# Moving the right-hand SBUF pools of a hybrid encoder layer by 160 bytes

## The chip, the cores and the metric

The kernel runs on one core of a Trainium2 chip. The metric is the device time of one execution in microseconds (us). The time before is 2487.82 us, the median of three runs (2487.3 to 2491.13 us).

## What is computed

One encoder layer on x of 1024 tokens and 1024 channels, all in float32. An RMSNorm is followed by one wide projection (10,016 columns of `w_in`, 1024 rows); its columns feed three branches, each a scan in both directions: a state-space branch (SSD), an RWKV-7 branch and an HGRN2 branch. Each branch is projected to 1024 channels, the three are merged with sigmoid gates, and an output projection and a residual addition follow. Then come RMSNorm, a SwiGLU feed-forward part with 2816 inner channels, another residual addition and a last RMSNorm.

```python
p = rmsnorm(x, norm1_w) @ w_in
z, xbc, dt_raw, p_rwkv, p_hgrn, p_gate = split(p)
mixed = g0 * (ssd(...) @ w_branch_ssm) + g1 * (rwkv7(...) @ w_branch_rwkv) + g2 * (hgrn2(...) @ w_branch_hgrn)
x = x + mixed @ w_out
h_gate, h_up = split(rmsnorm(x, norm2_w) @ ffn_w_in)
x = x + (silu(h_gate) * h_up) @ ffn_w_down
out = rmsnorm(x, final_norm_w)
```

## The kernel before

**A product in three matmuls.** Every large float32 product is made of three fp32r matmuls. Each operand is split into a high part (a cast on ACT) and a low part (the difference, on DVE or POOL), and high times high, high times low and low times high are added up in PSUM. `mm3` (L226 to L232), `Jobs.steps` (L329 to L331) and `rows_mm` (L1572 to L1578) issue them. In `matmul(ps, a, b)` the first operand is loaded into TensorE as weights, 128 columns, and the second streams through it, 512 columns. In the profile, a matmul `out<-in,in` names the streaming operand first.

**Stages.** Until about 1500 us the scans run, with the first projections filling TensorE between them (`Jobs`, which the FILL table portions out; its matmuls are L329 to L331). Then:
- merges (`merges`, L1461 on): branch projections, L230 to L232, whose results are gated and added
- output projection (`out_proj`), 384 matmuls, L1576 to L1578, each row group followed by a sum on DVE and a square on ACT; from its second half transposes for the next stage are mixed in (L1601)
- up stage (`Ffn.up`): for each of 22 column blocks f, seven block products (Strassen-Winograd) in the order 1, 2, 6, 7, 5, 4, 3, each of 12 matmuls (L1576 to L1578). The weight blocks are split just ahead of their use (L1740 on ACT, L1741 on DVE), the sums of products go through DVE
- down stage (`Ffn.down`): seven products over six groups of inner channels, 924 matmuls on the same lines. DVE splits the weight blocks and the activation blocks (L1793) and adds each product into an accumulator (L1915); the last group also makes the final norm.

A planner, which simulates the program while it is built, sets the order of the instructions on each engine; a wait is added wherever an instruction touches a buffer that another has to finish with first, also where two pools use the same bytes one after the other.

**Where the operands lie.** SBUF is given out by pools, each with one row of bytes per partition. Pools grow from the left end, or from the right end with `side="right"`. The right end is byte 229,344, which is 224 modulo 256. The pools that hold matmul operands, with their first byte and this modulo 256:

| pool | side | first byte | modulo 256 | holds |
|---|---|---|---|---|
| wpool | left | 20032 | 64 | weights of the projections (wh, wl), raw weights |
| gtp | left | 48704 | 64 | gb blocks of the up stage, raw tiles |
| ring0, ring1 | left | 65088, 97856 | 64 | operands of merges and output projection (oh, ol) |
| ffl | left | 79424 | 64 | xb of products 6, 7, 4 |
| dn | left | 79424 | 64 | ab blocks, accumulators |
| stpool | right | 223552 | 64 | on128 and other masks, staging tiles |
| xpool | right | 158016 | 64 | the normed input x, split |
| r32 | right | 196576 | 224 | rb blocks, gates, two operands of the merges (or) |
| mpool0, mpool1 | right | 163808, 131040 | 224 | mx; then xb of products 1, 2, 5, 3 |

All tiles in these pools that matmuls read have sizes that are multiples of 2048 bytes, and a block inside them starts at a multiple of 512 bytes, so an operand keeps its pool's offset modulo 256. stpool and xpool are closed at the end of the first projections; r32 and the mpools are opened at their place. on128 is a byte mask of 1025 columns, for which 1056 bytes are set aside; all of stpool takes 5792 bytes.

So, before, the weights and the streaming operand meet like this (offset of streaming operand, offset of weights): first projections 64, 64; merges 64, 64, but 224, 64 for `or`; output projection 64, 224; up stage, from the second f on, 224, 64 for products 1 and 2, 64, 224 for products 6, 7 and 4, and 224, 224 for products 5 and 3; down stage 224, 64.

Of the kernel before, what the change touches and what calls it, by code (L numbers as in the profile page):

```python
# [9 lines left out]
F32 = mybir.dt.float32  # L10
F32R = mybir.dt.float32r
U8 = mybir.dt.uint8
# [6 lines left out]
P = 128  # L19
L = 1024  # L20
# [32 lines left out]
def setup_consts(g, tp):  # L53
    nc, A = g.nc, g.A
    cp = g.cpool
    ident = cp.tile([P, P], F32, tag="ident", name="ident")
    nc.gpsimd.memset(ident, 1.0)
    nc.gpsimd.affine_select(out=ident, in_=ident, pattern=[[1, P]], compare_op=ALU.is_equal,
                            fill=0.0, base=0, channel_multiplier=-1)
    g.ident = ident  # L60

    def tri(name, op, base, cm, step, scale=1.0):
        t = cp.tile([P, P], F32, tag=name, name=name)
        nc.gpsimd.memset(t, scale)
        nc.gpsimd.affine_select(out=t, in_=t, pattern=[[step, P]], compare_op=op, fill=0.0,
                                base=base, channel_multiplier=cm)
        return t

    g.tri = tri
    g.tri_le = tri("tri_le", ALU.is_ge, 0, -1, 1)  # L70
    g.tri_ge = tri("tri_ge", ALU.is_ge, 0, 1, -1)


    bd = tp.tile([P, P], F32, tag="bd", name="bd")
    nc.gpsimd.memset(bd, 0.0)
    nc.gpsimd.memset(bd[0:64, 0:64], 1.0)
    nc.gpsimd.memset(bd[64:128, 64:128], 1.0)
    ones = tp.tile([P, P], F32, tag="ones", name="ones")
    nc.gpsimd.memset(ones, 1.0)
    g.bd, g.ones = (cp.tile([P, P], F32R, tag=n, name=n) for n in ("bd", "ones"))  # L80
    nc.gpsimd.tensor_scalar(g.bd, bd, 1.0, None, MUL)
    nc.gpsimd.tensor_scalar(g.ones, ones, 1.0, None, MUL)

    col = cp.tile([P, 8], F32, tag="col", name="col")
    for i, v in enumerate((1.0, NORM_EPS, 1e-12, LN_EPS)):
        nc.gpsimd.memset(col[:, i:i + 1], v)
    g.c_one, g.c_eps, g.c_12, g.c_ln = (col[:, i:i + 1] for i in range(4))

    g.vec = {}


def vector_rows(g, pool, tag, groups, queue):

    out = []
    for gi, grp in enumerate(groups):
        rows = pool.tile([P, P], F32, tag=f"rows{tag}{gi}", name=f"rows{tag}{gi}")
        o = 0
        for name, src, k in grp:
            queue.dma_start(rows[o:o + k, :], src)
            o += k  # L100
        out.append((f"{tag}{gi}", rows, grp))
    return out


def vector_cols(g, loaded):

    nc = g.nc
    for tag, rows, grp in loaded:
        n = sum(e[2] for e in grp)
        ps = g.mmps.tile([P, 512], F32, tag="mm", name="vps")  # L110
        nc.tensor.transpose(ps[:, :n], rows[:n, :], g.ident[:n, :n])
        cols = g.cpool.tile([P, n], F32, tag=f"vcols{tag}", name=f"vcols{tag}")
        nc.vector.tensor_copy(cols, ps[:, :n])
        o = 0
        for name, src, k in grp:
            g.vec[name] = cols[:, o:o + k]
            o += k
# [74 lines left out]
def rms_rows(g, xt, junk, xn, st):  # L192

    nc = g.nc
    nc.scalar.activation(junk, xt, AF.Square, accum_out=st[:, 0:1])
    nc.scalar.activation(st[:, 1:2], st[:, 0:1], AF.Sqrt, bias=g.c_eps, scale=1.0 / D)
    nc.vector.reciprocal(st[:, 0:1], st[:, 1:2])
    nc.vector.tensor_scalar(xn, xt, st[:, 0:1], None, MUL)


def transpose_split(g, x, half, xs, wcols, new, psum=None):

    nc = g.nc
    for k in range(KT):
        ps = (psum or g.mmps).tile([P, 512], F32, tag="mm", name="tps")
        for j in range(4):
            nc.tensor.transpose(ps[:, j * P:(j + 1) * P], xs[j][:, k * P:(k + 1) * P], g.ident)
        hi, lo = new(half, k)
        nc.scalar.activation(hi, ps, AF.Identity, scale=wcols[:, k:k + 1])
        nc.vector.scalar_tensor_tensor(lo, ps, wcols[:, k:k + 1], f32(hi), MUL, SUB)  # L210
        x.add(half, hi, lo)
# [172 lines left out]
def rwkv(g):  # L384
# [38 lines left out]
    with tc.manual_schedule(engines={ACT}):  # L423
        J.first(0)
    derived_vectors(g)
    level_masks(g)

    keep = ExitStack()
# [534 lines left out]
def level_masks(g):  # L963
    nc = g.nc

    on = g.on128 = g.stpool.tile([P, L + 1], U8, tag="on128", name="on128")
    nc.gpsimd.memset(on, 1)
    nc.gpsimd.memset(on[:, 0:L].rearrange("p (c t) -> p c t", t=P)[:, :, 0:1], 0)
    nc.gpsimd.memset(on[:, L:L + 1], 0)


    t2 = g.stpool.tile([P, 3, 64], F32, tag="st", name="blk", bufs=2)
    blk, blk2 = t2[:, 0], t2[:, 1]
    msk = g.msk = g.stpool.tile([P, 6, 64], U8, tag="msk", name="msk")
    g.id64 = g.stpool.tile([P, 64], F32, tag="id64", name="id64")
    for b in range(2):
        nc.gpsimd.tensor_scalar(g.id64[b * 64:b * 64 + 64], g.ident[b * 64:b * 64 + 64, b * 64:b * 64 + 64],
                                1.0, None, MUL)


    def blocks(t, n):
        nc.gpsimd.memset(t, 1.0)
        for b in range(2):
            if n < 64:
                v = t[b * 64:b * 64 + 64].rearrange("p (a b) -> p a b", b=n)

                nc.gpsimd.affine_select(out=v, in_=v, pattern=[[-n, 64 // n], [0, n]], compare_op=ALU.is_ge,
                                        fill=0.0, base=0, channel_multiplier=1)
                nc.gpsimd.affine_select(out=v, in_=v, pattern=[[n, 64 // n], [0, n]], compare_op=ALU.is_ge,
                                        fill=0.0, base=n - 1, channel_multiplier=-1)  # L990
    blocks(blk, 64)
    for i, h in enumerate(LEV[1:]):
        blocks(blk2, h)
        nc.vector.tensor_sub(msk[:, i], blk, blk2)
        nc.vector.tensor_copy(blk, blk2)
# [971 lines left out]
def start(es, tc, A):  # L1967
    g = Ctx()
    g.tc, g.nc, g.A = tc, tc.nc, A
    nc = tc.nc  # L1970
    g.wraw_bufs = 2
    g.lo_eng = nc.gpsimd
    g.wq = nc.scalar
    g.cpool = es.enter_context(tc.tile_pool(name="const", bufs=1))
    g.dram = es.enter_context(tc.tile_pool(name="scr", bufs=1, space=DRAM))
    g.mmes = es.enter_context(ExitStack())
    g.mmps = g.mmes.enter_context(tc.tile_pool(name="mmps", bufs=3, space=PSUM))
    g.wpool = es.enter_context(tc.tile_pool(name="wpool", bufs=2))
    g.xes = es.enter_context(ExitStack())
    g.stpool = g.xes.enter_context(tc.tile_pool(name="stpool", bufs=1, side="right"))  # L1980
    g.xpool = g.xes.enter_context(tc.tile_pool(name="xpool", bufs=1, side="right"))
    x = g.x = Split()

    def new(half, k):
        return [g.xpool.tile([P, 512], F32R, tag=f"x{half}{k}{i}", name="x1") for i in "hl"]

    g.n1 = ExitStack()
    tp = g.n1.enter_context(tc.tile_pool(name="n1", bufs=1))
    nc.scalar.preload_act_table_set("sqrt_and_others")
    xs = [tp.tile([P, D], F32, tag="xt", name="xt", bufs=NT) for _ in range(NT)]  # L1990

    def load(half):
        for t in range(half * 4, half * 4 + 4):
            nc.sync.dma_start(xs[t], A["x"][0, t * P:(t + 1) * P, :])

    def rows(half):
        for t in range(half * 4, half * 4 + 4):
            junk = tp.tile([P, D], F32, tag="junk", name="junk", bufs=2)
            st = tp.tile([P, 2], F32, tag="st", name="st", bufs=4)
            rms_rows(g, xs[t], junk, xs[t], st)  # L2000

    def trans(half):
        with tc.tile_pool(name="n1ps", bufs=4, space=PSUM) as pp:
            transpose_split(g, x, half, xs[half * 4:half * 4 + 4], g.vec["norm1_w"], new, pp)

    g.x_load, g.x_rows, g.x_trans = load, rows, trans
    load(0)
    setup_consts(g, tp)
    n1w = vector_rows(g, tp, "n", [[("norm1_w", A["norm1_w"].rearrange("o (k p) -> (o k) p", p=P), 8)]], nc.scalar)
    vector_cols(g, n1w)  # L2010
    g.n1pool = tp
    return g


@with_exitstack
def layer_kernel(ctx, tc, A, out):
    g = start(ctx, tc, A)
    J = g.J = Jobs(g)

# [101 lines left out]
```

## Time and profile before

| | |
|---|---|
| median of three runs | 2487.82 us |
| the profiled execution | 2489.66 us |
| its span, first to last instruction | 2487.9 us |
| PE busy | 2332.5 us, 94% of the span |
| DVE busy | 1635.9 us, 66% |
| ACT busy | 988.9 us, 40% |
| POOL busy | 1068.9 us, 43% |
| granted TensorE clock, mean | 0.964 of full speed |

PE is TensorE's matmul part and PEld its weight loads, which run beside it; DVE is VectorE, ACT ScalarE, POOL GpSimd. Matmuls are pipelined, and a matmul's end is modelled: its "duration" overlaps the next matmul's, so the rate is read from the starts, or from the number of weight loads in a stretch that is full. The granted clock has two levels, 1.0 (2.4 GHz) and 0.5 (1.2 GHz).

### The profile page before, as it was taken

What the parts mean: (1) busy time and instruction counts of PE and PEld (TensorE: products, weight loads), DVE (VectorE), ACT (ScalarE), POOL (GpSimd) and SP (SyncE); (2) the same over time, 40 slices, a digit from 0 to 9 for tenths busy, and PEclk for the clock granted to TensorE, in tenths of its full rate; (3) what the DMA queues carried; (4) which work ended last, traced back from release to release, by engine and by line L of the source; (5) the groups of instructions that cost most, each with busy time, mean ns of one, the idle gap of its engine ahead of it and who ended that gap; (6) DMA issues with size and microseconds to landing.
All of it is one profiled execution on the core that took longest, in us unless ns stands there. A gap on an engine that the chain in (4) does not pass through costs nothing.

```text
span 2487.9 us, 37793 instructions
## 1 busy us (share of the span) xinstructions
PE 2332.5 (94%) x14785; PEld 1870.3 (75%) x14785; DVE 1635.9 (66%) x2130; ACT 988.9 (40%) x1460; POOL 1068.9 (43%) x862
## 2 busy tenths in 40 slices
PE   8998999999989889999899899999899999999995
PEld 6776788888867677778568667788688888877764
DVE  5688862456566866846666776553774454469999
ACT  6544532222464653436135235332433333344333
POOL 4433422344044533420751761421454444447885
PEclk9998999899999999999899999999999999999998
DMA  5455685655342232225645647531132222253321
GB/s 149 126 145 131 164 209 139 189 164 149 118 138 91 77 109 77 68 88 172 140 125 172 142 128 250 189 115 72 60 102 81 80 84 78 85 172 109 102 67 68
DMA packets 381215, 306.27 MB, mean 123 GB/s; under 512 B 111273, under 2 KB 323149, under 8 KB 381037
## 3 DMA queue, kind: packets, MB, share of 16 engines
q1 hardware_dynamic: 260909, 225.71, 30.6%
q10 hardware_dynamic: 119936, 77.61, 10.7%
q8 instruction: 117, 1.92, 0.3%
q0 software_dynamic: 192, 0.52, 0.1%
q14 instruction: 61, 0.50, 0.1%
HBM read 209.68 MB, written 94.11 MB: 122 GB/s over the span
## 4 chain that ended last, share of the span: by engine, by line
PE 59%; DVE 23%; POOL 5%; issue 5%; DMA 4%; ACT 3%; SPq 0%; ACTq 0%; DVEq 0%; POOLq 0%
PE mm L329 6%; PE mm L330 6%; PE mm L331 6%; PE ps L1577 6%; PE ps L1576 6%; PE ps L1578 6%; DVE acc L1915 3%; DVE ab L1793 2%; PE Gps L802 2%; PE mm L232 2%; PE mm L230 2%; PE mm L231 2%; DMA E<-cumd 2%; POOL E L1357 2%; DVE rb L1793 2%
## 5 line engine op out<-in xcount | busy, mean ns | idle before, releaser
L329 PE MATMUL mm<-x,wh 128*128 128x512 f32 (+1 forms) x1232 | 500.0, 406 | 0.5 <-ACT wh L220 0.5
L330 PE MATMUL mm<-x,wh 128*128 128x512 f32 (+1 forms) x1232 | 497.2, 404 | 0.0
L331 PE MATMUL mm<-x,wl 128*128 128x512 f32 (+1 forms) x1232 | 495.0, 402 | 0.8 <-DVE wl L222 0.7
L329 PEld LDWEIGHTS mm<-x,wh 128*128 128x128 f32 (+1 forms) x1232 | 234.5, 190 | 62.2 <-issue 10.6
L331 PEld LDWEIGHTS mm<-x,wl 128*128 128x128 f32 (+1 forms) x1232 | 234.7, 190 | 57.2 <-issue 6.0
L330 PEld LDWEIGHTS mm<-x,wh 128*128 128x128 f32 (+1 forms) x1232 | 234.8, 191 | 55.9 <-issue 6.8
L1577 PE MATMUL ps<-xb,rb 128*128 128x512 f32 x432 | 171.1, 396 | 0.0
L1576 PE MATMUL ps<-xb,rb 128*128 128x512 f32 x432 | 170.1, 394 | 0.0
L1578 PE MATMUL ps<-xb,rb 128*128 128x512 f32 x432 | 169.9, 393 | 0.0
L220 ACT CAST wh<-wr 128x1024 fp32r<-128x1024 f32 (+2 forms) x103 | 100.3, 974 | 125.1 <-PE mm L330 102.4
L222 POOL TENSOR_TENSOR wl<-wr,wh 128x1024 fp32r<-128x1024 f32 x30 | 78.2, 2606 | 149.2 <-ACT wh L220 140.0
L1576 PE MATMUL ps<-rb,ab 128*128 128x512 f32 x308 | 127.4, 414 | 14.3 <-DVE acc L1915 13.5
L222 DVE TENSOR_TENSOR wl<-wr,wh 128x1024 fp32r<-128x1024 f32 (+2 forms) x73 | 98.1, 1343 | 64.6 <-ACT wh L220 64.5
L1577 PE MATMUL ps<-rb,ab 128*128 128x512 f32 x308 | 125.3, 407 | 2.3 <-POOL rb L1793 2.3
L1578 PE MATMUL ps<-rb,ab 128*128 128x512 f32 x308 | 124.1, 405 | 1.5 <-DVE ab L1793 1.5
L1740 ACT CAST rb<-fs 128x512 fp32r<-128x512 f32 x85 | 52.5, 621 | 172.1 <-PE ps L1578 119.7
L271 ACT COPY st<-mm 128x512 f32<-128x512 f32 x130 | 75.5, 581 | 95.1 <-PE mm L331 76.0
L805 DVE TENSOR_TENSOR Gc<-Gps,mk 128x256 f32<-128x256 f32 x64 | 27.0, 423 | 112.4 <-PE Gps L802 58.6
L1576 PEld LDWEIGHTS ps<-xb,rb 128*128 128x128 f32 x432 | 81.2, 188 | 19.9
L1578 PEld LDWEIGHTS ps<-xb,rb 128*128 128x128 f32 x432 | 81.2, 188 | 19.0
L1577 PEld LDWEIGHTS ps<-xb,rb 128*128 128x128 f32 x432 | 81.1, 188 | 18.9
L1357 POOL TENSOR_TENSOR E<-E,cums 128x1024 f32<-128x1024 f32 x32 | 68.3, 2146 | 60.3 <-DMA E<-cumd 54.5
(503 smaller groups left out, 5584.8 us busy)
## 6 DMA issues: line engine op xcount, KB each, us to landing
wr<-in_w_in_dram ACTq DMA_DIRECT2D x74, 512.0 KB
fr<-in_ffn_w_in_dram SPq DMA_DIRECT2D x44, 512.0 KB
E<-cumd SPq DMA_DIRECT2D x32, 512.0 KB
pg<-st ACTq DMA_DIRECT2D x48, 256.0 KB
gt<-pg SPq DMA_DIRECT2D x24, 512.0 KB
ad<-a SPq DMA_DIRECT2D x22, 512.0 KB
dr<-in_ffn_w_down_dram SPq DMA_DIRECT2D x22, 512.0 KB
ar<-ad SPq DMA_DIRECT2D x22, 512.0 KB
```

What stands on the lines that cost most here:

```text
L220: nc.scalar.copy(hi[:, :kt, :n], raw[:, :kt, :n])
L222: g.lo_eng.tensor_sub(lo[:, :kt, :n], raw[:, :kt, :n], f32(hi[:, :kt, :n]))
L271: g.nc.scalar.copy(st[:n], ps)
L329: g.nc.tensor.matmul(ps[:n], w[0][:, k, :n], xh, start=(k == 0), stop=False)
L330: g.nc.tensor.matmul(ps[:n], w[0][:, k, :n], xl, start=False, stop=False)
L331: g.nc.tensor.matmul(ps[:n], w[1][:, k, :n], xh, start=False, stop=(k == KT - 1))
L1357: nc.gpsimd.tensor_tensor(e, e, cs.unsqueeze(2).broadcast_to([P, 8, P]), SUB)
L1576: nc.tensor.matmul(ps, ah, bh, start=(i == 0), stop=False)
L1577: nc.tensor.matmul(ps, ah, bl, start=False, stop=False)
L1578: nc.tensor.matmul(ps, al, bh, start=False, stop=(i == n - 1))
L1793: eng.tensor_sub(blk[:, 1], s, f32(blk[:, 0]))
L1915: nc.vector.tensor_add(m[j], m[j], ps)
```

## The change

Two edits. A pool of 160 bytes is opened at the right end ahead of all other right-hand pools, and it stays open; one column of it is set to zero by a POOL memset. The mask tile on128 is allocated with 1408 columns instead of 1025, and the first 1025 are used as before.

```diff
@@ def level_masks(g):
-    on = g.on128 = g.stpool.tile([P, L + 1], U8, tag="on128", name="on128")
+    on = g.on128 = g.stpool.tile([P, L + 384], U8, tag="on128", name="on128")[:, 0:L + 1]
     nc.gpsimd.memset(on, 1)
@@ def start(es, tc, A):
     g.wpool = es.enter_context(tc.tile_pool(name="wpool", bufs=2))
+
+    rp = es.enter_context(tc.tile_pool(name="rightpad", bufs=1, side="right"))
+    nc.gpsimd.memset(rp.tile([P, 40], F32, tag="pad", name="pad")[:, 0:1], 0.0)
     g.xes = es.enter_context(ExitStack())
     g.stpool = g.xes.enter_context(tc.tile_pool(name="stpool", bufs=1, side="right"))
     g.xpool = g.xes.enter_context(tc.tile_pool(name="xpool", bufs=1, side="right"))
```

## Rows read from the trace of the kernel before

**Rows 1.** The page: span, busy time of the engines, granted clock in 40 slices.

```profile
span 2487.9 us, 37793 instructions
...
PE 2332.5 (94%) x14785; PEld 1870.3 (75%) x14785; DVE 1635.9 (66%) x2130; ACT 988.9 (40%) x1460; POOL 1068.9 (43%) x862
...
PEclk9998999899999999999899999999999999999998
```

**Rows 2.** Busy time by stretch (start:end, length, busy us and count, clock, DMA).

```profile
66.52:106.05 39.53, 39.53 (x175) 32.67 (x174) 24.17 (x17) 20.78 (x27) 17.95 (x15) 1.00 0.24 64
...
1501.37:1532.91 31.54, 31.54 (x140) 26.09 (x139) 17.41 (x24) 14.19 (x17) 0.00 (x0) 1.00 0.78 277
1570.22:1675.60 105.38, 105.38 (x460) 86.13 (x459) 50.81 (x54) 36.27 (x44) 31.06 (x23) 1.00 0.42 134
1675.69:1736.82 61.13, 61.13 (x263) 49.13 (x262) 20.55 (x33) 12.65 (x30) 7.84 (x5) 1.00 0.24 89
...
1774.48:1804.99 30.51, 23.97 (x93) 17.05 (x92) 30.23 (x36) 16.41 (x29) 19.38 (x12) 0.83 0.18 52
1804.99:2215.52 410.53, 410.53 (x1764) 331.37 (x1763) 214.19 (x303) 128.50 (x212) 183.71 (x130) 1.00 0.28 90
...
2255.00:2415.00 160.00, 151.18 (x608) 116.02 (x607) 159.88 (x189) 57.34 (x103) 133.75 (x86) 0.97 0.30 96
```

The five busy times are those of PE, PEld, DVE, ACT and POOL in this order.

**Rows 3.** The chain that ended last, by line: up stage, then output projection.

```profile
by line: PE ps L1577 33.5%; PE ps L1576 33.3%; PE ps L1578 33.2%
...
by line: PE mm L1576 30.7%; PE mm L1577 30.4%; PE mm L1578 30.0%; PE tps L1601 3.5%; PE ps L1578 1.9%; PE ps L1577 1.8%; PE ps L1576 1.8%
```

**Rows 4.** The same chain in the down stage, 2215 us to the end.

```profile
by line: DVE acc L1915 23.8%; DVE ab L1793 22.8%; DVE rb L1793 14.2%; issue 8.5%; DVE acc L1949 5.4%; POOL dt L1802 4.4%; POOL as L1837 3.2%; POOL acc L1919 3.1%; DVE acc L1954 2.1%; DVE as L1837 2.1%; DMA ar<-ad 1.8%; POOL rb L1793 1.7%; A
```

**Rows 5.** PE in order of time in the up stage: start, length, instruction.

```profile
1886.05 0.40 PE L1576 MATMUL ps<-xb,gb 128*128 128x512 f32 x1
...
1888.85 0.40 PE L1576 MATMUL ps<-xb,rb 128*128 128x512 f32 x1
...
1900.04 0.40 PE L1576 MATMUL ps<-xb,rb 128*128 128x512 f32 x1
...
1901.89 0.39 PE L1578 MATMUL ps<-xb,rb 128*128 128x512 f32 x1
...
1902.80 0.39 PE L1576 MATMUL ps<-xb,gb 128*128 128x512 f32 x1
```

**Rows 6.** PE's groups in the down stage: busy, mean ns, idle before them and releaser.

```profile
L1576 PE MATMUL ps<-rb,ab 128*128 128x512 f32 x308 | 127.4, 414 | 14.3 <-DVE acc L1915 13.5
L1577 PE MATMUL ps<-rb,ab 128*128 128x512 f32 x308 | 125.3, 407 | 2.3 <-POOL rb L1793 2.3
L1578 PE MATMUL ps<-rb,ab 128*128 128x512 f32 x308 | 124.1, 405 | 1.5 <-DVE ab L1793 1.5
```

**Rows 7.** DVE's splits of the up stage by tile: duration min/median/max, first and last start.

```profile
L1741 DVE TENSOR_TENSOR gb<-fr,gb x43: 679/694/1783, 1789.4 to 2163.5; 128x512 fp32r<-128x512 f32 x43
...
L1741 DVE TENSOR_TENSOR rb<-fr,rb x23: 679/693/1783, 1675.9 to 2186.0; 128x512 fp32r<-128x512 f32 x23
```

**Rows 8.** POOL's first instructions in order of time, and the chain's first pieces.

```profile
3.41 0.11 POOL L403 MEMSET pt<- 128x1 f32 x1
3.44 0.11 POOL L404 MEMSET pt<- 128x1 f32 x1
...
2.68 7.73 DMA wr<-in_w_in_dram
...
13.46 1.11 PE tps L207 x4
```

**Rows 9.** PE in order of time in the down stage, around one hole.

```profile
2265.41 0.50 PE L1576 MATMUL ps<-rb,ab 128*128 128x512 f32 x1 [2.54 <-DVE acc L1915]
...
2266.55 0.63 PE L1577 MATMUL ps<-rb,ab 128*128 128x512 f32 x1
...
2269.53 0.50 PE L1578 MATMUL ps<-rb,ab 128*128 128x512 f32 x1
```

## The prediction

> **What bounds the kernel now.** I read the page first: one core, span 2487.9 us in an execution of 2489.66 us, against a median of 2487.82 us of three runs; PE is busy for 94% of the span, and its granted clock is at the full level in nearly every slice [rows 1]. So the kernel is a matmul stream, and the question is where this stream stands still and how fast it goes where it doesn't. The second view, busy time by stretch, answers both [rows 2]. In the up stage of the feed-forward part PE is busy for 410.53 of 410.53 us at full clock, and DVE has half its time free (214.19 us); the chain through that stretch is PE alone, 100% [rows 3]. The two stretches of the merges and the output projection that end at 1736.82 us are full too, and the projection's chain is PE for nine tenths. In the down stage it is the other way round: DVE is busy for 159.88 of 160.00 us and PE has holes; its chain names DVE's accumulations and splits first [rows 2, 4].
>
> Now the rate. All matmuls named here have the same form (128x128 weights, 128x512 columns, fp32r), one weight load each, so the number of weight loads in a stretch counts them. At full clock and without a hole, a matmul takes, from rows 2:
> - first projections, xpool against wpool: 39.53 us / 174 = 227.2 ns
> - merges, ring against wpool: 31.54 / 139 = 226.9 ns
> - output projection, ring against mpool: 61.13 / 262 = 233.3 ns
> - up stage: 410.53 / 1763 = 232.9 ns.
>
> The mean durations of groups (405 to 414 ns [rows 6]) hide this, because pipelined matmuls overlap; only the spacing of the starts tells. Beside it I put the memory map: left-hand pools and xpool start at byte 64 modulo 256, r32 and the two mpools at 224. The fast stretches pair 64 with 64, the slow ones 64 with 224. The up stage holds both kinds in one place: products 1, 2, 6, 7 and 4 pair the two offsets, products 5 and 3 pair 224 with 224. Product 2 of one f goes from 1886.05 to 1888.85 us, 12 matmuls, 233 ns each. Product 3 starts at 1900.04 and the next product at 1902.80: its first eight take 1.85 us (231 ns), its last four 0.91 us (227.5 ns) [rows 5]. So a shared offset gives 227 ns at 224 as well as at 64, and the delay of a mixed pair reaches some matmuls into the next product. I take it that the moving operand of one matmul and the weight load of the next read SBUF at the same time and disturb each other by their relative place.
>
> **The change, part by part.** *Pad.* 160 bytes at the right end put r32 and both mpools 160 bytes lower: 196576, 163808 and 131040 become 196416, 163648 and 130880, all 64 modulo 256. *Wider mask tile.* on128 grows from 1056 to 1408 bytes as allocated, so stpool from 5792 to 6144; with the pad, xpool moves by 512 bytes and stays at 64. The first projections keep their 227 ns, and all pairs above then share 64.
>
> *Up stage:* 1763 x (232.9 - 227.0) = 10.3 us. All of it is on the path, since PE is 100% of the chain; what is late next, DVE, has 196 us in hand.
> *Output projection:* 262 x (233.3 - 227.0) = 1.65 us to 1736.82 us; the remaining 122 of its 384 matmuls lie among transposes in the next stretch, at the same saving 0.8 us. PE holds that chain too.
> *Merges:* 96 matmuls stream two tiles that lie in r32; their stretch gives 105.38 / 459 = 229.6 ns, so 459 x 2.6 = 1.2 us.
> *Stretch from 1774.48 to 1804.99 us:* DVE 30.23 of 30.51 us; a faster matmul gives nothing. Taken at 0.
> *Down stage:* its 924 matmuls pair 224 with 64 and would give 924 x 6.5 = 6.0 us if PE set the pace. It does not: DVE does nearly no waiting, and PE waits 18.1 us for others [rows 2, 6]. A faster matmul makes PE wait longer for DVE's accumulation, which is late next. Between 0 and 6.0 us I take 0.3 us, near the lower end, because the DVE row is full.
> DVE's splits and additions there start when the last up products give their buffers back, so what is saved before 2215 us is not lost at that border.
>
> *Added memset* of one column on POOL: such a memset takes 0.11 us, starts 0.03 us before the next, and stands before the identity that the first transposes need; they start at 13.46 us, behind a weight load from HBM of 7.73 us [rows 8]. Cost nothing; without that cover 0.1 us at most. The mask's memsets still write 1025 bytes. *Buffers at new places:* an r32 tile spanned parts of three xpool tiles and now spans two exactly, so its first load can only wait for fewer readers; bound 0 to 1 us of gain, taken at 0. *DVE, ACT and POOL* on the moved tiles: the split into gb (64) and into rb (224) has a median of 694 and 693 ns [rows 7]; I take 0.
>
> Sum: 10.3 + 1.65 + 0.8 + 1.2 + 0.3 = 14.2 us. From the profiled execution, 2489.66 us, this gives 2475.4; it lies 1.84 us above the median, so from the median 2473.6 us.
>
> One rule speaks against all this. The rows show 233 and 227 ns for one form at one clock. The Trainium skill, "TensorE: Matmul & The Clock Gate", section "Step-by-step: what each phase is for", says that TensorE reads the moving operand and the next weights through two independent ports, so that loading weights takes nothing from the running matmul. By it no address could matter and the sum would be 0. The trace does not agree, 227 against 233 ns.
>
> **Rivals.**
> - *The gain is only partial.* If products in the up stage with one offset stay at the 230 ns that product 3 averages (2.76 us / 12), the up stage gives 1763 x 2.9 = 5.1 us and the rest about half, 1.9 us: 2480.8 us. For: the products at 224 never had a whole 227 ns average. Against: their last four do, and whole stretches at 64.
> - *Nothing changes.* The spacing comes with the stage, not the offset (say, the traffic of the other engines beside it), and the two reads of TensorE do not meet: 2487.8 us. For: the trace shows no address. Against: both rates inside one product sequence of the up stage. This is the outcome that the Trainium skill's page "TensorE: Matmul & The Clock Gate" stands for.
> - *The down stage gains as well*, since DVE is released earlier by each PSUM bank: the other 5.7 us too, 2467.9 us. Against: the full DVE row.
> - *Slower: the clock in the down stage.* With matmuls 6.5 ns shorter, PE's holes grow. After a hole of 2.54 us, ended by DVE at 2265.41, the clock falls, and from 2266.55 to 2269.53 us seven matmuls stand 427 ns apart instead of 234: 1.4 us [rows 9]. The mean clock there is 0.97 now. To end 5 us slower the kernel would need (14.2 + 5) / 1.4, some 14 more such falls; at 17 it would be at 2497 us. Each hole grows by 0.08 us only (12 matmuls), so I hold it for unlikely.
> - The instruction order may also come out differently, as a planner sets it and one POOL instruction is new; the trace can't price this. I let it widen the range.
>
> **How the numbers follow.** Within 0.2% means within 5.0 us, about what a measurement of this kernel can tell from no change. Forecast 0.62, partial 0.15, down stage too 0.07: faster 0.84. No change 0.11. Slower, by the clock or another order, 0.05. The range goes from 2466, just beyond the case with the down stage, to 2483, below which the partial case lies; it leaves out the case of no change and the slower one.
>
> **What would show it.** Right: the up stage at 227 ns, about 400 us for 1763 matmuls; the output projection at 227; the first projections unchanged at 227; the down stage as long as now (272 us from the last up product to the end) with more PE idle behind DVE's accumulation. Wrong: the up stage at 230 or above (partial), any stretch of xpool against wpool off 227 ns, or a down stage longer by microseconds with a lower clock. If the up stage is 400 us and the time still doesn't fall by 12 us, the down stage or a new order took it back.

## The result and the profile after

The changed kernel takes 2472.72 us (median of six runs, 2469.6 to 2476.17), against 2487.69 us before, measured beside it: 15.0 us less, a ratio of 0.9938 with a 95% interval of 0.9925 to 0.9951. The forecast was 2473.6 us.

The profiled execution took 2473.65 us. The page's head, against [rows 1]:

```profile
span 2471.9 us, 37794 instructions
...
PE 2309.0 (93%) x14785; PEld 1865.5 (75%) x14785; DVE 1633.4 (66%) x2130; ACT 989.0 (40%) x1460; POOL 1070.9 (43%) x863
```

One instruction more, the memset; PE is busy for 23.5 us less and its weight loads for 4.8 us less, the other engines within 2.5 us of before. Busy time by stretch comes next, the stretches of [rows 2] at their new times; the columns are PE, PEld, DVE, ACT and POOL, then granted clock and DMA.

```profile
67.90:107.43 39.53, 39.53 (x175) 32.66 (x174) 24.18 (x17) 20.78 (x27) 17.96 (x15) 1.00 0.23 64
1499.53:1531.10 31.57, 31.57 (x140) 26.10 (x139) 17.40 (x24) 14.11 (x17) 0.00 (x0) 1.00 0.78 273
1568.13:1672.52 104.39, 104.39 (x460) 86.40 (x459) 49.48 (x54) 36.27 (x44) 32.27 (x23) 1.00 0.44 137
1672.52:1731.92 59.40, 59.40 (x263) 49.13 (x262) 18.92 (x33) 12.75 (x30) 9.97 (x5) 1.00 0.25 92
1768.93:1799.45 30.52, 24.56 (x93) 17.86 (x92) 30.23 (x36) 16.43 (x30) 19.51 (x13) 0.78 0.18 52
1799.45:2199.06 399.61, 399.61 (x1764) 331.00 (x1763) 215.31 (x303) 128.55 (x212) 183.36 (x129) 1.00 0.29 93
2199.06:2471.94 272.88, 225.38 (x926) 174.74 (x924) 265.58 (x324) 106.34 (x208) 206.28 (x132) 0.94 0.29 99
```

Read each row as length over weight loads. The first projections take 39.53 us for 174 matmuls, to the hundredth what they took before, 227.2 ns. The output projection now needs 59.40 / 262 = 226.7 ns instead of 233.3, the up stage 399.61 / 1763 = 226.7 ns instead of 232.9. PE fills these stretches as before; it is full at a higher rate, and the chain through the up stage is still PE alone:

```profile
by line: PE ps L1576 33.4%; PE ps L1578 33.3%; PE ps L1577 33.3%
```

The last row, the down stage to the end, is within half a microsecond of what it was: 272.88 us, against 272.42 us before, whose row is

```profile
2215.52:2487.94 272.42, 230.76 (x926) 177.01 (x924) 265.16 (x323) 106.23 (x208) 206.77 (x132) 0.93 0.30 99
```

In order of time, the products of the up stage no longer show an uneven spacing. These are the starts around the border of two products:

```profile
1880.60 0.39 PE L1577 MATMUL ps<-xb,gb 128*128 128x512 f32 x1
1880.83 0.39 PE L1578 MATMUL ps<-xb,gb 128*128 128x512 f32 x1
1881.06 0.39 PE L1576 MATMUL ps<-xb,rb 128*128 128x512 f32 x1
1881.28 0.39 PE L1577 MATMUL ps<-xb,rb 128*128 128x512 f32 x1
1881.51 0.39 PE L1578 MATMUL ps<-xb,rb 128*128 128x512 f32 x1
```

Four steps take 0.91 us, across a change from gtp's weights to r32's, where only the last matmuls of a product in [rows 5] were that quick.

Where did the down stage's share go? PE's groups there, which answer to [rows 6]:

```profile
L1576 PE MATMUL ps<-rb,ab 128*128 128x512 f32 x308 | 125.8, 408 | 20.1 <-DVE acc L1915 19.1
L1577 PE MATMUL ps<-rb,ab 128*128 128x512 f32 x308 | 122.4, 397 | 2.4 <-POOL rb L1793 2.4
L1578 PE MATMUL ps<-rb,ab 128*128 128x512 f32 x308 | 121.5, 397 | 1.5 <-DVE ab L1793 1.5
```

The idle time ahead of L1576 rose from 14.3 to 20.1 us, and what ends it is DVE's accumulation, 19.1 us instead of 13.5. PE's busy time in the stage fell from 230.76 to 225.38 us, by 5.4 us, and over the three groups PE waits 24.0 us instead of 18.1, 5.9 us longer: the gain turned into a wait.

Between the profiled executions the books are: scans and first projections 2.1 us shorter (1483.66 to 1481.52 us at the first merge), merges 191.57 to 190.55 (1.0 us), output projection from the end of the merges to 1774.48 us before and 1768.94 us after, 99.26 to 96.86 us (2.4 us), the stretch behind it unchanged, up stage 10.9 us, down stage 0.5 us longer; in sum 16.0 us. The first 2.1 us are not counted for the change: no operand pair there has a new distance, and over the six kernels of this study whose xpool lies at wpool's offset the first merge starts anywhere from 1474.2 to 1483.7 us in the profiles. That leaves 13.9 us for the change, and the interval of the ratio, some 12 to 19 us, holds both them and the 15.0 us of the medians. Of these, the 1.0 us of the merges is the least certain: over the eight kernels of this study that hold the layer, the merges as a whole take 189.8 to 191.6 us in no order of the change; only their full stretch tells, 105.4 to 105.5 us in the three kernels that stream `or` from 224 and 104.0 to 104.6 us in the four in which `or` shares its weights' offset. The planner's order hardly moved: PE's 14785 matmuls come in the same order in both traces, by the names of their tiles, and so do DVE's instructions; on ACT two instructions changed places with a neighbour.

### The profile page after: what moved, and what is told of

Its sections match the earlier page's. It is cut to its first block, busy times and chain, and to the rows that moved or that the text cites. A ratio compares the mean times of both kernels' runs of the same rounds, so it can differ in the third digit from the quotient of the medians.

```text
span 2471.9 us, 37794 instructions
## 1 busy us (share of the span) xinstructions
PE 2309.0 (93%) x14785; PEld 1865.5 (75%) x14785; DVE 1633.4 (66%) x2130; ACT 989.0 (40%) x1460; POOL 1070.9 (43%) x863
## 4 chain that ended last, share of the span: by engine, by line
PE 60%; DVE 23%; POOL 5%; issue 5%; DMA 4%; ACT 3%; ACTq 0%; SPq 0%; DVEq 0%; POOLq 0%
PE mm L329 6%; PE mm L330 6%; PE mm L331 6%; PE ps L1576 6%; PE ps L1577 6%; PE ps L1578 6%; DVE acc L1915 3%; DVE ab L1793 2%; PE Gps L802 2%; PE mm L232 2%; PE mm L230 2%; PE mm L231 2%; DMA E<-cumd 2%; POOL E L1357 2%; DVE rb L1793 1%
## 5 line engine op out<-in xcount | busy, mean ns | idle before, releaser
L329 PEld LDWEIGHTS mm<-x,wh 128*128 128x128 f32 (+1 forms) x1232 | 234.1, 190 | 61.7 <-issue 10.6
L1578 PE MATMUL ps<-xb,rb 128*128 128x512 f32 x432 | 168.1, 389 | 0.0
L1576 PE MATMUL ps<-xb,rb 128*128 128x512 f32 x432 | 168.0, 389 | 0.0
L1577 PE MATMUL ps<-xb,rb 128*128 128x512 f32 x432 | 168.0, 389 | 0.0
L1576 PE MATMUL ps<-rb,ab 128*128 128x512 f32 x308 | 125.8, 408 | 20.1 <-DVE acc L1915 19.1
L1577 PE MATMUL ps<-rb,ab 128*128 128x512 f32 x308 | 122.4, 397 | 2.4 <-POOL rb L1793 2.4
L1578 PE MATMUL ps<-rb,ab 128*128 128x512 f32 x308 | 121.5, 397 | 1.5 <-DVE ab L1793 1.5
L1915 DVE TENSOR_TENSOR acc<-acc,ps 128x512 f32<-128x512 f32 x148 | 94.1, 675 | 0.2 <-PE ps L1578 0.2
L1576 PEld LDWEIGHTS ps<-xb,rb 128*128 128x128 f32 x432 | 81.1, 188 | 16.9
```

Source lines behind the costliest of these rows:

```text
L329: g.nc.tensor.matmul(ps[:n], w[0][:, k, :n], xh, start=(k == 0), stop=False)
L1576: nc.tensor.matmul(ps, ah, bh, start=(i == 0), stop=False)
L1577: nc.tensor.matmul(ps, ah, bl, start=False, stop=False)
L1578: nc.tensor.matmul(ps, al, bh, start=False, stop=(i == n - 1))
L1915: nc.vector.tensor_add(m[j], m[j], ps)
```

## The experiments

The theory at this point: the streaming operand of a matmul and the weight load beside it disturb each other unless their SBUF offsets agree modulo 256. The main rivals: the place of r32 and the mpools counts and not the relation; no offset counts at all; and, for the down stage, that it did gain.

**Streams alone.** A kernel with nothing but matmuls, in place of the layer:

```python
SEGS = [((0,), (0,)), ((32,), (0,)), ((64,), (0,)), ...
        ((0, 160), (0, 160)), ((0, 160), (160, 0))]
...
for i in range(90):
    u, v = a[i % len(a)] // 4, b[i % len(b)] // 4 + 128 * (i % 4)
    nc.tensor.matmul(ps, ws[:, v:v + 128], mv[:, u:u + 512], start=(i == 0), stop=(i == 89))
```

> A kernel of its own that leaves the whole layer out: 13 segments of 90 fp32r matmuls (128x128 weights, 128x512 columns) without a hole, nothing beside them on the other engines. The streaming operand starts a number of bytes past the weights' offset modulo 256: 0, 32, 64, 96, 128, 160, 192, 224, then again 0; then 160/160 (both moved), 0/160; then two segments that alternate, one in which a matmul's own operands share an offset and the next weights do not, one the other way round. Theory (the stream meets the next weights' load at their relative place): 227 ns at 0 and at 160/160, about 234 at 160, 96 and 0/160; the segment with shared own operands 234, the one whose next weights share the offset 227. Rival 1 (a matmul's own pair counts): the last two segments the other way round. Rival 2 (no offset counts, the other engines' traffic does): all segments alike.

Busy time by segment (PE, PEld, ACT, POOL), 90 weight loads each (89 in the last row); the segments are 0, 32, 64, 96, 128, 160, 192, 224, again 0, 160/160, 0/160 and the two alternating ones:

```profile
17.14:37.54 20.40, 20.40 (x91) 16.89 (x90) 0.00 (x0) 0.00 (x0) 1.00 0.00 1
37.54:58.54 21.00, 21.00 (x91) 16.87 (x90) 0.59 (x1) 0.00 (x0) 1.00 0.00 1
58.54:79.14 20.60, 20.60 (x91) 16.90 (x90) 0.59 (x1) 0.00 (x0) 1.00 0.00 0
79.14:100.15 21.01, 21.01 (x91) 16.89 (x90) 0.59 (x1) 0.00 (x0) 1.00 0.00 1
100.15:121.15 21.00, 21.00 (x91) 16.90 (x90) 0.59 (x1) 0.00 (x0) 1.00 0.00 1
121.15:142.23 21.08, 21.08 (x91) 16.95 (x90) 0.59 (x1) 0.00 (x0) 1.00 0.00 0
142.23:163.22 20.99, 20.99 (x91) 16.92 (x90) 0.59 (x1) 0.00 (x0) 1.00 0.00 1
163.22:184.21 20.99, 20.99 (x91) 16.90 (x90) 0.59 (x1) 0.00 (x0) 1.00 0.00 1
184.21:204.63 20.42, 20.42 (x91) 16.89 (x90) 0.59 (x1) 0.00 (x0) 1.00 0.00 1
204.63:225.07 20.44, 20.44 (x91) 16.89 (x90) 0.59 (x1) 0.00 (x0) 1.00 0.00 0
225.07:246.08 21.01, 21.01 (x91) 16.90 (x90) 0.59 (x1) 0.00 (x0) 1.00 0.00 1
246.08:267.14 21.06, 21.06 (x91) 16.90 (x90) 0.59 (x1) 0.00 (x0) 1.00 0.00 1
...
267.14:287.61 20.47, 20.47 (x90) 16.68 (x89) 0.59 (x1) 0.00 (x0) 1.00 0.00 0
```

Distance 0 gives 20.40 / 90 = 226.7 ns, wherever both lie (160/160: 227.1); 32, 96, 128, 192 and 224 give 233 ns, 160 gives 234; 64 stands apart with 228.9. No other engine does anything beside a copy of 0.59 us, so the traffic of other engines is not needed for it, and that rival falls. The two alternating segments settle less: with shared own operands and mixed next weights a matmul takes 234.0 ns, so sharing an offset with its own weights is not enough; but with shared next weights it takes 20.47 / 89 = 230.0 ns and not the 227 that the theory wanted. There the starts stand 236 and 224 ns apart in turn, and neither is the spacing of a shared pair. The next load counts more than the own; what the other 3 ns are stays open.

**The pad alone.**

```diff
--- the changed kernel
-    on = g.on128 = g.stpool.tile([P, L + 384], U8, tag="on128", name="on128")[:, 0:L + 1]
+    on = g.on128 = g.stpool.tile([P, L + 1], U8, tag="on128", name="on128")
```

> The pad without the wider mask tile: r32 and the mpools share 64 with the left-hand pools, but xpool goes to 160 and meets the weights of the first projections at 64. Theory (the relation counts): from the first merge to the end as in the changed kernel, some 13 to 14 us shorter than before; the first projections go from 227 to about 233 ns, 3792 matmuls x 6 ns = 23 us if all were on the path, 15 to 23 us as PE is nearly full there: in sum 2489 to 2497 us. Rival (what counts is that r32 and the mpools are at 64): 2473 us, as the changed kernel.

2478.59 us, ratio 0.9966 (0.9952 to 0.9981). Its stretches: first projections, output projection, up stage.

```profile
66.24:106.84 40.60, 40.60 (x175) 32.67 (x174) 24.69 (x18) 20.80 (x27) 17.91 (x15) 1.00 0.24 66
1676.62:1736.01 59.39, 59.39 (x263) 49.13 (x262) 18.91 (x33) 12.79 (x30) 9.97 (x5) 1.00 0.25 92
1803.58:2203.19 399.61, 399.61 (x1764) 330.89 (x1763) 215.93 (x303) 128.97 (x212) 183.60 (x130) 1.00 0.29 93
```

The first projections go to 40.60 / 174 = 233.3 ns, as the theory had it and against the rival, and the later stages are the changed kernel's. But the total is only 6 us above that kernel's instead of 15 to 23, and below the 2489 to 2497 us that were expected.

**The mask tile alone.**

```diff
--- the changed kernel
-    rp = es.enter_context(tc.tile_pool(name="rightpad", bufs=1, side="right"))
-    nc.gpsimd.memset(rp.tile([P, 40], F32, tag="pad", name="pad")[:, 0:1], 0.0)
```

> The wider mask tile without the pad: r32 and the mpools stay at 224, xpool goes to 224 as well and meets the weights at 64. Theory: the later stages as before, the first projections at about 233 ns: 15 to 23 us slower than before, 2503 to 2511 us. Rival (the mask tile alone does nothing): 2488 us.

2497.04 us, slower than before: 1.0031 (1.0018 to 1.0044). The wider mask is no harmless byte mask: without the pad it moves xpool off its partner.

```profile
68.65:109.40 40.75, 40.75 (x175) 32.76 (x174) 24.73 (x18) 20.82 (x27) 17.87 (x15) 1.00 0.25 66
1685.17:1746.31 61.14, 61.14 (x263) 49.13 (x262) 18.86 (x33) 12.71 (x30) 9.99 (x5) 1.00 0.24 89
1814.24:2224.77 410.53, 410.53 (x1764) 331.35 (x1763) 214.20 (x303) 128.86 (x212) 183.83 (x130) 1.00 0.28 90
```

234 ns in the first projections, the later stages within 0.01 us of before. Again the total moved by less than expected, 9 us instead of 15 to 23. Where the rest went shows in everything ahead of the first merge, in the kernel before, the changed one, the pad alone and the mask alone (busy time of PE, PEld, DVE, ACT, POOL):

```profile
0.00:1483.66 1483.66, 1383.52 (x10762) 1115.82 (x10762) 972.69 (x1288) 628.94 (x858) 587.82 (x544) 0.96 0.48 133
...
0.00:1481.52 1481.52, 1379.62 (x10761) 1112.81 (x10761) 971.73 (x1288) 629.07 (x858) 587.48 (x545) 0.96 0.48 133
...
0.00:1486.33 1486.33, 1391.49 (x10761) 1107.23 (x10761) 972.14 (x1288) 630.05 (x858) 587.68 (x545) 0.97 0.48 133
...
0.00:1494.84 1494.84, 1398.88 (x10761) 1112.68 (x10761) 968.34 (x1288) 629.77 (x858) 591.52 (x544) 0.97 0.48 132
```

PE's idle time shrinks as its matmuls get longer: 101.9 us in the changed kernel, 94.8 with the pad alone; 100.1 before, 96.0 with the mask alone. Its busy time grows by 11.9 and 15.4 us. PE's order is the same in all four, so the starts can be set side by side as well. Where two first-projection matmuls follow each other without a hole, some 3300 of the 3792, the step grew by 5.6 ns with the pad alone and by 6.1 ns with the mask alone, 18.4 and 20.1 us in sum; the first merge came only 4.8 and 11.2 us later, and these two carry the scatter of the scans. So most of the 23 us was there, and much of it filled waits for the scans that were there anyway. That PE is 93% busy in a stretch did not mean that 93% of a matmul's time is on the path.

**One offset by another road.**

```diff
--- the kernel before
+    lp = es.enter_context(tc.tile_pool(name="leftpad", bufs=1))
+    nc.gpsimd.memset(lp.tile([P, 40], F32, tag="pad", name="pad")[:, 0:1], 0.0)
     g.wpool = es.enter_context(tc.tile_pool(name="wpool", bufs=2))
...
-    on = g.on128 = g.stpool.tile([P, L + 1], U8, tag="on128", name="on128")
+    on = g.on128 = g.stpool.tile([P, L + 128], U8, tag="on128", name="on128")[:, 0:L + 1]
```

> The other way to one offset: no pad at the right, but 160 bytes at the left end, and a mask tile 96 bytes larger than before, so that all pools with matmul operands start at 224 modulo 256. Theory (only the relation counts): 2473 us as the changed kernel, all dense stretches at 227 ns. Rival (the place itself counts, 64 is good and 224, which no 64 bytes divide, is not): the up stage at 230 ns and the first projections at 230 as well: 3792 x 3 = 11 us slower there and 5 us faster later, about 2494 us.

2471.62 us, 0.9937 (0.9914 to 0.9959), the changed kernel's time. First projections and up stage:

```profile
66.63:106.20 39.57, 39.57 (x175) 32.67 (x174) 24.16 (x17) 20.82 (x27) 17.95 (x15) 1.00 0.23 64
1798.88:2198.49 399.61, 399.61 (x1764) 331.00 (x1763) 215.87 (x303) 128.95 (x212) 183.65 (x130) 1.00 0.29 93
```

The same 227 ns with every operand at 224: the relation counts, and between 64 and 224 the place does not.

**Only the down stage mixed.**

```diff
--- the changed kernel, Ffn.down
         self.fp = fp
+        dp = fp.tile([P, 40], F32, tag="dpad", name="dpad")
+        nc.gpsimd.memset(dp[:, 0:1], 0.0)
```

> The changed kernel, with 160 bytes set aside at the start of the down stage's pool: its activation blocks lie at 224 again and meet r32 at 64, so the down stage alone is mixed as before the change. Theory (DVE sets the pace there): its matmuls are 234 ns apart again in dense stretches, and the stage from the last up product to the end takes 272 to 273 us as in both kernels; 2472 to 2474 us. Rival (the down stage's matmuls were worth their time): 924 x 6.5 ns = 6 us slower, 2479 us.

2473.28 us, 0.9939 (0.9923 to 0.9955), no slower than the changed kernel within its spread. The down stage to the end, and PE's first group in it (two inserted lines make DVE's accumulation L1917):

```profile
2200.07:2473.39 273.32, 229.78 (x926) 174.97 (x924) 265.73 (x324) 106.18 (x208) 207.38 (x133) 0.94 0.29 99
...
L1576 PE MATMUL ps<-rb,ab 128*128 128x512 f32 x308 | 127.2, 413 | 16.3 <-DVE acc L1917 15.0
```

PE is busy for 4.4 us longer than in the changed kernel and waits 3.8 us less ahead of L1576, and the stage has the same length within half a microsecond. Its dense steps are 233.2 ns apart (the distance is 96 here, 160 before), against 227.8 in the changed kernel and 234.1 before, by the starts. DVE sets the pace there; the rival's 6 us are not there. Over the eight kernels that hold the layer, three of them with these operands at one offset, the stage takes 272.3 to 273.5 us with no order by the offset.

**A distance of 128.**

```diff
--- the changed kernel
-    on = ....tile([P, L + 384], ...
+    on = ....tile([P, L + 256], ...
-    nc.gpsimd.memset(rp.tile([P, 40], ...
+    nc.gpsimd.memset(rp.tile([P, 8], ...
```

> The change with a pad of 32 bytes, and a mask tile that keeps xpool at 64: r32 and the mpools lie at 192, 128 away from the left-hand pools. By the streams alone a distance of 128 costs as much as 160 (233.4 against 234.3 ns). Theory (the offset counts modulo 256, and a distance of 128 is as bad): up stage at 233 ns, 2486 to 2488 us, as before. Rival (a distance of half the 256 bytes is as good as none, only smaller units count): 2473 us.

2485.35 us, 0.9986 (0.9975 to 0.9998): a small gain, not the changed kernel's. Output projection and up stage:

```profile
1673.57:1734.45 60.88, 60.88 (x263) 49.33 (x262) 18.88 (x33) 12.66 (x30) 9.97 (x5) 1.00 0.25 90
1802.49:2210.78 408.29, 408.29 (x1764) 331.40 (x1763) 214.33 (x303) 128.60 (x212) 183.56 (x130) 1.00 0.28 91
```

The time lies 0.7 us under the range that was expected, far from the rival. 408.29 / 1763 = 231.6 ns against 232.9 before: a distance of 128 is nearly as bad as those of 160 and 96, so it is no matter of half the 256 bytes. By the starts, some four tenths of the small gain lie in products 5 and 3, which share their offset in both kernels: they average 227.9 and 228.4 ns here and 230.1 and 230.0 before, as behind a mixed product they come to 226.7 ns after three matmuls here and after nine there.

**The mpools alone.**

```diff
--- the kernel before
+    mp = ctx.enter_context(tc.tile_pool(name="midpad", bufs=1, side="right"))
+    nc = tc.nc
+    nc.gpsimd.memset(mp.tile([P, 40], F32, tag="pad", name="pad")[:, 0:1], 0.0)
     g.mes = ctx.enter_context(ExitStack())
```

> A pad of 160 bytes between r32 and the mpools in the kernel before: the mpools go to 64, r32 stays at 224. Theory: the output projection gets 227 ns (2.4 us less, as in the changed kernel); in the up stage products 1 and 2 gain their shared offset and products 5 and 3 lose it, so 60 of 84 matmuls stay mixed and the stage stays at 410 us; merges and down stage as before: 2485 to 2486 us. Rival (the place of the mpools counts, not the pair): the products that stream from them, 48 of 84, at 227 ns, the up stage 6 us shorter: 2479 us.

2483.84 us, 0.9985 (0.9975 to 0.9996), some 1 us under the range that was expected. Output projection and up stage:

```profile
1664.49:1723.89 59.40, 59.40 (x263) 49.15 (x262) 18.84 (x33) 12.66 (x30) 9.97 (x5) 1.00 0.25 92
1791.36:2200.36 409.00, 409.00 (x1764) 330.92 (x1763) 214.77 (x303) 128.58 (x212) 183.61 (x130) 1.00 0.28 90
```

The output projection gets its 227 ns; the up stage stays at 409.00 us, for as many products lost a shared offset as won one, and not near the 404.5 us of the rival. The starts in this trace show both the delay that a mixed product leaves behind and the part of the next weights (means over 20 of the 22 f). Product 1, now shared but behind a mixed one, averages 229.9 ns; product 2 behind it keeps 226.7 ns for eleven matmuls, and only its last, whose next weights lie in r32 at 224, takes 236.6 ns. (This profiled execution took 2475.27 us, the shortest of ten; its scans ended early, as the times in the window show. The stretches are what to read, not the total.)

**Streams once more.**

> Streams as in the first run, the layer left out again, with distances 0, 4, 16, 48, 64, 80, 128, 256, 320 bytes, then 64/160; then a streaming operand that alternates between 0 and 160 against fixed weights, fixed streaming operand against alternating weights, and own pairs shared while the next differ by 64. Theory (only the distance modulo 256 counts): 256 like 0 (226.7 ns), 320 like 64 (228.9 ns), 64/160 like 160 (234 ns); 4, 16, 48, 80 between 229 and 234 ns; the alternating ones halfway, about 230 ns. Rival (16-byte or 64-byte units count): 64 and 128 both at 226.7 and 16 like 0.

Distances 0, 4, 16, 48, 64, 80, 128, 256 and 320:

```profile
18.01:38.40 20.39, 20.39 (x91) 16.89 (x90) 0.00 (x0) 0.00 (x0) 1.00 0.00 1
38.40:59.70 21.30, 21.30 (x91) 16.88 (x90) 0.59 (x1) 0.00 (x0) 1.00 0.00 1
59.70:80.54 20.84, 20.84 (x91) 16.92 (x90) 0.59 (x1) 0.00 (x0) 1.00 0.00 0
80.54:101.54 21.00, 21.00 (x91) 16.99 (x90) 0.59 (x1) 0.00 (x0) 1.00 0.00 1
101.54:122.15 20.61, 20.61 (x91) 16.90 (x90) 0.59 (x1) 0.00 (x0) 1.00 0.00 1
122.15:142.95 20.80, 20.80 (x91) 16.88 (x90) 0.59 (x1) 0.00 (x0) 1.00 0.00 0
142.95:163.95 21.00, 21.00 (x91) 16.90 (x90) 0.59 (x1) 0.00 (x0) 1.00 0.00 1
163.95:184.37 20.42, 20.42 (x91) 16.89 (x90) 0.59 (x1) 0.00 (x0) 1.00 0.00 1
184.37:204.99 20.62, 20.62 (x91) 16.90 (x90) 0.59 (x1) 0.00 (x0) 1.00 0.00 1
```

256 is like 0 and 320 like 64: the distance counts modulo 256. Four bytes are the worst of all that were tried, 21.30 / 90 = 236.7 ns, past the 234 ns that were expected as the upper end; 16 bytes cost 231.6 and 80 bytes 231.1. The segment 64/160 took 234.2 ns like 160 (204.99 to 226.07 us). The three alternating segments came to 232.2, 231.8 and 231.7 ns where about 230 was expected. The mean over the two distances to the next weights, from the segments of one distance, would be 230.4, 230.1 and 231.1 ns; it falls short of them by 0.6 to 1.8 ns, and where that comes from stays open.

## Why the prediction was right

Step by step, the forecast term first, then the measured one:
- Up stage 10.3 us: 10.9 us. The term took 227.0 ns for the shared offset and the stretch runs at 226.7; PE alone is on the path there, so all of it arrived.
- Output projection 2.45 us (both stretches): 2.4 us. Merges 1.2 us: 1.0 us, with the scatter said above; their matmul rate in the full stretch is 104.39 / 459 = 227.4 ns.
- Stretch behind the output projection 0: 30.52 against 30.51 us, DVE-bound as read.
- Down stage 0.3 us: -0.5 us, within the scatter of that stage, and the experiment that mixed it again found no loss. Taking 0.3 out of 0 to 6.0 us, because the DVE row was full, was the choice that mattered most; with all 6.0 the forecast would have been 2468 us.
- Memset, new buffer places, other engines' work on moved tiles at 0: nothing in the runs speaks against it, and PE's and DVE's order is the same. These were not priced one by one.

Sum 14.2 us forecast, 13.9 us found in the stages, 15.0 us between the medians, of which the rest lies within the scatter of the scans. That the total came within 0.9 us of the forecast is in part chance: the scans alone scatter by more.

The rivals: the partial gain (230 ns in the products at 224) fell with the up stage at 226.7 ns; its 230 ns were the delay carried over from the mixed product ahead, as the last four matmuls in [rows 5] had hinted and products 1 and 2 of the mpools alone show. "Nothing changes" fell with the streams alone. The Trainium skill, "TensorE: Matmul & The Clock Gate", section "Step-by-step: what each phase is for", says that loading the next weights takes no read bandwidth from the running matmul. It names no address; in the streams alone an address changes the rate from 226.7 to 233 or 234 ns with nothing else at work, and the measurement decides. The clock rival did not show: the granted clock of the down stage is 0.94 in the changed kernel and in the one whose down stage alone is mixed, and was 0.93 before.

One statement of the mechanism went too far: that the streaming operand meets the next weights' load, and nothing else. The alternating segments show that the next weights matter more than the own, but not that they are all. That the two reads disturb each other in SBUF is argued from this; the runs show the dependence on the offsets and not the place where the time is lost.

Two expectations after the prediction missed in size: a mixed offset in the first projections cost 6 and 9 us, not 15 to 23. The step that failed there was to let PE's busy share stand for its share of the path: by the starts the matmuls took 18.4 and 20.1 us more, and the waits for the scans took up much of it.

## What to carry to other kernels

Where a dense stream of matmuls loads new weights for each one, take the spacing of the starts in a full stretch (length over weight loads) and compare stretches of one form; a few per cent between them can be the operands' SBUF offsets modulo 256, which pools that grow from the two ends of SBUF easily get different. (The runs show it for fp32r matmuls of 128x128 weights and 512 columns with a weight load each, and for nothing else.) Make them agree with a pad, and look at every pool that the pad moves: the same pad without its counterpart gave back 6 of 15 us here. Count the gain only where PE alone is the chain; where another engine's row is full it turns into a wait.

## What the runs showed of the hardware that was not expected

Of the distances tried, all multiples of 4 bytes, one of 4 bytes modulo 256 costs the most (236.7 ns against 226.7), and 64 bytes ahead is nearly free (228.9 ns) while 192, 64 the other way, is not (20.99 us for its 90 matmuls, 233.2 ns). Why the sign counts stays open. Behind a run of mixed pairs, shared pairs need up to nine matmuls until they keep their 226.7 ns (product 5 before the change, by the starts). Where the first merge starts differs by 9.5 us between profiled executions of kernels that have the same offsets up to there, while the up stage takes the same 399.61 us in the four kernels that share one offset there; a stage's own length told more than the totals could.
